# Two-block sequence model: the end of the first channel mixer worked off by token halves, its sums of squares taken on four column groups

## The chip, the core and the metric

The kernel runs on one core of a Trainium2 chip. The metric is the device time of one execution in microseconds (us), and the figure for a kernel is the median of its runs. The core has a matrix engine (TensorE, PE in the profile; its weight loads are PEld), a vector engine (VectorE, DVE), a scalar engine (ScalarE, ACT), a general engine (GpSimd, POOL), and SyncE (SP), whose queue issues most of the transfers. Each engine works through its own instructions in a fixed order and waits for others by semaphores.

## The reference, cut to what matters

```python
x = first_block(...)   # token mixer, then channel mixer; 16 meta tokens + 1024 tokens, width 1024
y = second_block(x)    # rwkv / attention mixer, then channel mixer
# end of first_block's channel mixer, for 1024 tokens:
y = (gelu(a) * (h @ w_up)) @ w_down          # w_down: 2816 x 1024
x = x + rmsnorm(y, g_post)                   # mean of squares over the 1024 channels of a token
# start of second_block:
h = rmsnorm(x, mix_norm_gain)                # again a mean of squares over the channels
proj = h @ w_in                              # 1536 + 32 + 32 + 96 + 1536 columns
p = p_rwkv + (token_shift(p_rwkv) - p_rwkv) * shift_mix
```

Everything is float32.

## The kernel before

Channels lie on the 128 partitions and tokens along the free dimension, so the 1024 channels of a token are eight tiles `y[0]` to `y[7]` of 128 x 1024 tokens. A float32 product is made as three products in a reduced format (`mm3`, lines 196 to 198: high x high, low x high, high x low), so every operand is split into a high and a low part. A product writes 128 x 512 into a bank of PSUM, and most work goes by the two token halves of `CH2`, here the first half (tokens 0 to 511) and the second.

`down` (line 1153) multiplies by `w_down`. It takes the 22 tiles of 128 hidden channels two at a time; for both halves and all eight output tiles it makes 6 products of 128x512 into a bank, and VectorE adds the bank to `y[j]`. After the last pair the function `each` is called for every tile and half.

`ffn1` (line 1187) then makes the two norms. The sum of squares of a half is formed in two ways. For the first norm, ScalarE squares a tile, GpSimd adds the squares of tiles 0 to 6 up in `acc`, and `add_sums` (line 292) lets TensorE reduce the 128 partitions: four calls with a 128-token block of squares as weights and a single column of ones, so that the sums of tokens come to stand on partitions. `rstd` (line 299) makes the reciprocal root there with some 14 small VectorE instructions, spreads it over a diagonal (`rdg`), and multiplies it back to a row for all partitions with TensorE (line 318). Then follow for each tile of a half: scale by gain and root (VectorE, line 156), add the residual `x1` (GpSimd, line 149), high part of the next input (`xh`, ScalarE), its low part (`xl`, VectorE), the square of the new value and four calls of line 292 for the second norm, and the store to `dx2`. The second norm's root goes into `rs`.

The next stage starts on `xh` and `xl` without its norm, which is multiplied in behind the product: `shifted` (line 1297) projects one column tile (24 products for each half) and multiplies the bank by `rs`. `lora_in` calls it for two column tiles, of 128 and of 32 columns, here the first and the second column tile; `rkv` calls it for twelve more. In this block the projections have two banks.

The order of each engine is set by a scheduler at build time, which moves instructions past each other where data allow; a tile in a pool waits until the last user of its buffer is done.

Of the kernel before, what the change touches and what calls it, by code (L numbers as in the profile page):

```python
# [48 lines left out]
class Build:  # L49
# [1103 lines left out]
    def down(self, hid, w_down, y, last, each=None, after=None, between=None):  # L1153
# [14 lines left out]
        for f in range(0, NF, 2):  # L1168
            fs = [load(f), load(f + 1)]
            end = f == NF - 2  # L1170
            for a, b in last if end else CH2:
                for j in range(KD):
                    ps = self.mm_ps([P, b - a])
                    for i, (g, w) in enumerate(fs):
                        self.mm3(ps, (w[0][:, j, :], w[1][:, j, :]), (g[0][:, a:b], g[1][:, a:b]), i == 0, i == 1)
                    if f == 0:
                        nc.scalar.copy(y[j][:, a:b], ps)
                    else:
                        self.tt(y[j][:, a:b], y[j][:, a:b], ps, ALU.add)
                    if each and end:  # L1180
                        each(j, a, b)
                if after and end:
                    after(a, b)
            if between:
                between(f)

    def ffn1(self, fx):
# [4 lines left out]
        acc = self.slot([P, T2], name="acc", tag="WC")  # L1192
        self.dx2 = self.dram([KD, P, T2], "dx2")
        tot = {}

        def each(j, a, b):

            if j < KD - 1:
                self.square_acc(acc, y[j][:, a:b], j, a, b)
                return  # L1200
            if a not in tot:
                tot[a] = self.sums_ps()
                self.add_sums(tot[a], acc[:, a:b], True, False)
            self.square_sum(tot[a], y[j][:, a:b], False, True)

        self.down(hid, I["w_ffn_down"][0], y, CH2, each)
        rp = [self.rstd(tot[a], b - a, D) for a, b in CH2]
        self.rs = self.slot([P, T2], name="rs", tag="R")
        self.xh, self.xl = [], []
        for i, (a, b) in enumerate(CH2):  # L1210
            tot = self.sums_ps()
            for j in range(KD):
                if j % 2 == 0:
                    x1 = self.slot([P, 2, b - a], name="x1", tag="XE")
                    self.dma(out=x1, in_=self.dx1[j:j + 2, :, a:b].rearrange("j p t -> p j t"))
                if i == 0:
                    self.xh.append(self.slot([P, T2], F32R, "xh", "XH"))
                    self.xl.append(self.slot([P, T2], F32R, "xl", "XL"))
                h, l = self.xh[j][:, a:b], self.xl[j][:, a:b]
                t = y[j][:, a:b]  # L1220
                self.stt(t, t, gp[:, j:j + 1], rp[i], ALU.mult, ALU.mult)
                self.tt(t, t, x1[:, j % 2], ALU.add, eng=nc.gpsimd)
                self.act(h, t, AF.Copy, scale=gm[:, j:j + 1])
                self.stt(l, t, gm[:, j:j + 1], h.bitcast(F32), ALU.mult, ALU.subtract)
                self.square_sum(tot, t, j == 0, j == KD - 1)
                self.dma(out=self.dx2[j, :, a:b], in_=t)
            self.rstd(tot, b - a, D, self.rs[:, a:b])
        self.x = list(zip(self.xh, self.xl))

# [67 lines left out]
    def shifted(self, j0, m, mix):  # L1297

        w = self.wcol(self.I["w_in_2"][0], j0, m)
        p = self.slot([P, T2 + 1], name="p", tag="T")[:m]  # L1300
# [781 lines left out]
def block2(B):  # L2082
# [86 lines left out]
```

## Time and profile before

| | |
|---|---|
| time, median of 3 runs | 3236.83 us (3233.69 to 3240.65) |
| the profiled execution: time, span | 3233.1 us, 3231.4 us |
| mean granted TensorE clock | 0.941 of full speed |
| busy PE, PEld | 3009.3 us (93%), 2678.5 us (83%) |
| busy DVE, ACT, POOL | 2009.6 us (62%), 1142.4 us (35%), 1335.0 us (41%) |

The profile is of one execution. The span runs from its first to its last instruction. An engine's busy time is a share of the whole span, so it says little about one stage; the stretch at hand is the end of the first channel mixer, about 1555 to 1640 us. A granted clock of 1.00 is TensorE's upper level, 2.4 GHz, and 0.50 is its lower level, 1.2 GHz; a figure between them is a mean over a stretch with both.

### The profile page before, as it was taken

The page shows a single profiled execution, that of the slowest core. Times are in us where ns is not written, and L with a number is a line of the kernel's source. Part 1 is how long each engine was busy: PE and PEld are TensorE (multiplying, and loading weights), DVE is VectorE, ACT ScalarE, POOL GpSimd, SP SyncE. Part 2 cuts the span into 40 slices and gives each one's busy share as a digit, 9 for nine tenths or more (in the row PEclk, how much of TensorE's full clock was granted, in tenths as well). Part 3 has the DMA queues.
Part 4 walks back from the last instruction along what each step waited for, and adds up shares of the span by engine and source line. Part 5 has one row for each costly group of instructions (what it writes and reads, how often), then busy time and mean ns, then how long its engine had stood idle before and what let it go on. Part 6 is the DMA issues. An engine that isn't in the chain of part 4 may idle for free.

```text
span 3231.4 us, 52682 instructions
## 1 busy us (share of the span) xinstructions
PE 3009.3 (93%) x20614; PEld 2678.5 (83%) x20614; DVE 2009.6 (62%) x3618; ACT 1142.4 (35%) x2168; POOL 1335.0 (41%) x1291
## 2 busy tenths in 40 slices
PE   7999999989799999999999988788988899999998
PEld 6999998979799999877877776677778788887777
DVE  7556654674676666466776555558656766664666
ACT  3344313334343333311333323424444333334111
POOL 3767310033654444232532365543214744454430
PEclk9999999989799999999899989858998899999999
DMA  5333532335222222432223554533425122224321
GB/s 148 86 94 111 174 98 59 105 101 139 78 66 79 81 82 81 150 104 74 90 95 131 146 126 112 137 99 108 115 98 196 53 85 79 80 83 174 113 85 53
DMA packets 322535, 336.83 MB, mean 104 GB/s; under 512 B 60081, under 2 KB 270734, under 8 KB 322286
## 3 DMA queue, kind: packets, MB, share of 16 engines
q1 hardware_dynamic: 289646, 310.38, 31.0%
q10 hardware_dynamic: 32640, 23.08, 2.3%
q8 instruction: 162, 2.65, 0.3%
q14 instruction: 87, 0.71, 0.1%
HBM read 232.66 MB, written 96.40 MB: 102 GB/s over the span
## 4 chain that ended last, share of the span: by engine, by line
PE 61%; DVE 11%; POOL 7%; issue 5%; DMA 4%; ACT 2%; SPq 2%; ACTq 0%; DVEq 0%; POOLq 0%
PE pm L196 13%; PE pm L197 12%; PE pm L198 12%; PE px L197 5%; PE px L196 5%; PE px L198 5%; POOL fs L149 2%; POOL Z L149 2%; DVE dn L149 2%; SPq L142 2%; PE px L292 1%; DVE t L149 1%; PE pa L1877 1%; DMA M<-dm 1%; PE pc L1604 1%
## 5 line engine op out<-in xcount | busy, mean ns | idle before, releaser
L196 PE MATMUL pm<-xh,whi 128*128 128x512 f32 (+5 forms) x1344 | 446.9, 333 | 14.2 <-DVE th L149 11.5
L198 PE MATMUL pm<-xh,wlo 128*128 128x512 f32 (+5 forms) x1344 | 446.8, 333 | 0.0
L197 PE MATMUL pm<-xl,whi 128*128 128x512 f32 (+5 forms) x1344 | 446.4, 332 | 0.0
L149 DVE TENSOR_TENSOR y<-y,pm 128x512 f32<-128x512 f32 (+1 forms) x336 | 218.1, 659 | 159.4 <-PE pm L198 159.1
L196 PE MATMUL pm<-dn,dn 128*128 128x512 f32 (+1 forms) x736 | 286.0, 389 | 6.5 <-DVE y L149 6.2
L196 PEld LDWEIGHTS pm<-xh,whi 128*128 128x128 f32 (+1 forms) x1344 | 257.8, 192 | 35.8 <-DVE th L149 12.4
L197 PE MATMUL pm<-dn,dn 128*128 128x512 f32 (+1 forms) x736 | 282.4, 384 | 1.3 <-POOL dn L149 1.3
L198 PE MATMUL pm<-dn,dn 128*128 128x512 f32 (+1 forms) x736 | 282.5, 384 | 0.0
L197 PEld LDWEIGHTS pm<-xl,whi 128*128 128x128 f32 (+1 forms) x1344 | 257.6, 192 | 19.7 <-issue 0.9
L198 PEld LDWEIGHTS pm<-xh,wlo 128*128 128x128 f32 (+1 forms) x1344 | 257.8, 192 | 19.1 <-issue 0.5
L149 POOL TENSOR_TENSOR dn<-hid,dn 128x1024 fp32r<-128x1024 f32 x44 | 131.8, 3012 | 250.9 <-ACT dn L1161 250.9
L197 PE MATMUL px<-t,sh 128*128 128x258 f32 (+2 forms) x684 | 218.7, 320 | 6.9 <-DVE t L149 6.8
L196 PE MATMUL px<-t,sh 128*128 128x258 f32 (+2 forms) x684 | 217.2, 318 | 0.4 <-DVE gt L149 0.3
L198 PE MATMUL px<-t,sl 128*128 128x258 f32 (+2 forms) x684 | 216.1, 316 | 0.0
L149 DVE TENSOR_TENSOR wlo<-wraw,whi 128x1024 fp32r<-128x1024 f32 (+2 forms) x114 | 153.9, 1351 | 76.2 <-ACT whi L170 74.7
L196 PEld LDWEIGHTS pm<-dn,dn 128*128 128x128 f32 x736 | 138.2, 188 | 43.7 <-DVE y L149 14.2
L170 ACT CAST whi<-wraw 128x1024 fp32r<-128x1024 f32 (+2 forms) x114 | 103.4, 908 | 185.7 <-PE pm L197 154.8
L197 PEld LDWEIGHTS pm<-dn,dn 128*128 128x128 f32 x736 | 138.4, 188 | 29.9 <-POOL dn L149 1.7
L198 PEld LDWEIGHTS pm<-dn,dn 128*128 128x128 f32 x736 | 138.2, 188 | 30.0
L170 ACT CAST dn<-wd 128x1024 fp32r<-128x1024 f32 x44 | 46.1, 1048 | 290.8 <-PE pm L197 290.3
L197 PEld LDWEIGHTS px<-t,sh 128*128 128x128 f32 x684 | 131.3, 192 | 17.9 <-DVE t L149 9.1
L149 POOL TENSOR_TENSOR wraw<-wraw,par 128x1024 f32<-128x1024 f32 (+1 forms) x36 | 73.4, 2041 | 169.0 <-DMA wraw<-in_w_in_dram 128.7
(600 smaller groups left out, 8788.6 us busy)
## 6 DMA issues: line engine op xcount, KB each, us to landing
wraw<-in_w_in_dram SPq DMA_DIRECT2D x61, 512.0 KB
dhid<-up SPq DMA_DIRECT2D x44, 512.0 KB
wd<-in_w_ffn_down_dram SPq DMA_DIRECT2D x44, 512.0 KB
hid<-dhid SPq DMA_DIRECT2D x44, 512.0 KB
wra<-in_w_ffn_up_dram SPq DMA_DIRECT2D x33, 512.0 KB
wrb<-in_w_ffn_up_dram SPq DMA_DIRECT2D x33, 512.0 KB
dg<-th SPq DMA_DIRECT2D x16, 514.0 KB
wraw<-in_w_out_dram SPq DMA_DIRECT2D x16, 512.0 KB
```

What stands on the lines that cost most here:

```text
L142: self.nc.sync.dma_start(out=out, in_=in_)
L149: (eng or self.nc.vector).tensor_tensor(out=o, in0=a, in1=b, op=op)
L170: self.nc.scalar.copy(hi, src)
L196: nc.tensor.matmul(ps, a[0], b[0], start=start, stop=False, **kw)
L197: nc.tensor.matmul(ps, a[0], b[1], start=False, stop=False, **kw)
L198: nc.tensor.matmul(ps, a[1], b[0], start=False, stop=stop, **kw)
L292: self.nc.tensor.matmul(ps[:bw, i:i + 1], src[:, i * bw:i * bw + bw], self.ones[:, 0:1], start=start and i == 0, stop=stop and i == n - 1)
L1604: nc.tensor.matmul(ps, w[:, k], (yh, yl, yh)[q][:, a:b], start=i == 0, stop=i == 11)
L1877: nc.tensor.matmul(self.po[:, i - 4 * ch], pT[:, i * P - a:i * P - a + P], self.vx[j % 2][:, k].rearrange("p e v -> p (e v)")[:, 2 * e:2 * ...
```

## The change

In `down`, the last two pairs of hidden tiles are taken together where `each` is given: first both pairs for the first half, each in its own accumulation, then all four tiles in one accumulation of 12 products for the second half. `each` is so called for the first half while the second half's 96 products are still to come, and a new `after` makes the first half's root and scales its tiles there. The residual (`update`) of both halves stays behind `down`, and its addition goes from GpSimd to VectorE.

Squares are summed in another way for both norms (`square_quarter`): the weights are 32 columns of ones, the moving operand is the 128x512 square, and the result goes to 32 partitions of a bank at the column group 32*(j % 4), so that tiles 0 and 4 share a group. `quarters` copies that bank (ScalarE) and reduces it over the partitions with the four calls of line 292; the sum is 32 times too large, which the divisor 32*D takes back. GpSimd adds no squares up any more.

`shifted` takes several column tiles and goes by halves over all of them. `lora_in` takes its two tiles and the first tile of `rkv` in one call. The 32-column weights have their own loader (`narrow`), and `lora_in` stands ahead of `lora_weights`.

```diff
+        def chunk(fs, a, b, first, end):
+            for j in range(KD):
+                ps = self.mm_ps([P, b - a])
+                for i, (g, w) in enumerate(fs):
+                    self.mm3(ps, (w[0][:, j, :], w[1][:, j, :]), (g[0][:, a:b], g[1][:, a:b]), i == 0, i == len(fs) - 1)
...
+                if each and end:
+                    each(j, a, b)
+            if after and end:
+                after(a, b)
+
+        joint = 4 if each else 0
+        for f in range(0, NF - joint, 2):
...
+        if joint:
+            (a, b), *others = last
+            fs = [load(f) for f in (NF - 4, NF - 3)]
+            chunk(fs, a, b, False, False)
+            more = [load(f) for f in (NF - 2, NF - 1)]
+            chunk(more, a, b, False, True)
+            for a, b in others:
+                chunk(fs + more, a, b, False, True)
...
+        def scaled(j, a, b):
+            t = y[j][:, a:b]
+            self.stt(t, t, gp[:, j:j + 1], rp[a], ALU.mult, ALU.mult)
+
+        def update(j, a, b, x1, ps):
+
+            t = y[j][:, a:b]
+            self.tt(t, t, x1[:, j % 2], ALU.add)
+            h, l = self.xh[j][:, a:b], self.xl[j][:, a:b]
+            self.act(h, t, AF.Copy, scale=gm[:, j:j + 1])
+            self.stt(l, t, gm[:, j:j + 1], h.bitcast(F32), ALU.mult, ALU.subtract)
+            self.square_quarter(ps, t, j)
+            self.dma(out=self.dx2[j, :, a:b], in_=t)
 
         def each(j, a, b):
...
+            if j == 0:
+                sums[a] = self.q_ps([P, b - a])
+            self.square_quarter(sums[a], y[j][:, a:b], j)
+
+        def after(a, b):
+
+            rp[a] = self.rstd(self.quarters(sums[a]), b - a, 32 * D)
+            if a == 0:
+                for j in range(KD):
+                    scaled(j, a, b)
+
+        self.down(hid, I["w_ffn_down"][0], y, CH2, each, after)
...
+                if a:
+                    scaled(j, a, b)
+                update(j, a, b, x1, ps)
+            self.rstd(self.quarters(ps), b - a, 32 * D, self.rs[:, a:b])
         self.x = list(zip(self.xh, self.xl))
+
+    def square_quarter(self, ps, src, j):
+
+        n = src.shape[1]
+        sq = self.small([P, 512], tag="sq", bufs=self.nsq)[:, :n]
+        self.act(sq, src, AF.Square)
+        r = 32 * (j % 4)
+        self.nc.tensor.matmul(ps[r:r + 32], self.ones[:, :32], sq, start=j < 4, stop=j >= KD - 4, tile_position=(0, r))
+
+    def quarters(self, ps):
+
+        n = ps.shape[1]
+        s = self.small([P, 512], tag="sq", bufs=self.nsq)[:, :n]
+        self.nc.scalar.copy(s, ps)
+        tot = self.sums_ps()
+        self.add_sums(tot, s, True, True)
+        return tot
...
+    def shifted(self, *specs):
...
+        for c in CH2:
+            for (j0, m, _, _), w, p in zip(specs, ws, pp):
+                self.proj(w, self.x, [c], lambda ci, a, b, ps: self.tt(p[:, 1 + a:1 + b], ps, self.rs[:m, a:b], ALU.mult), m=m)
...
-        l1 = self.shifted(1536, P, self.par["mix_lora"][:, 0:1])
+        l1, l2, self.key0 = self.shifted((1536, P, self.par["mix_lora"][:, 0:1], "A"), (1664, 32, self.mixl[:, 0:1], "A"),
+                                         (512, P, self.par["mix"][:, 4:5], "T"))
...
+        B.lora_in()
         B.lora_weights()
-        B.lora_in()
```

Three places show what the scheduler makes of it on TensorE. The first is among the last products of `down`, in the kernel before (line 292: sums of the first half; `dn`: operands of `down`):

```order
L198 MATMUL pm_2047_16013<-dn_15867,dn_15870 128x512
L292 MATMUL px_2038_15960<-ones_71,acc_14331 128x1 x4
L292 MATMUL px_2038_15960<-ones_71,sq_15965 128x1 x4
L196 MATMUL pm_2045_16002<-dn_15855,dn_15857 128x512
L197 MATMUL pm_2045_16002<-dn_15856,dn_15857 128x512
```

The same place in the changed kernel, at the last tile of the second half (line 1259: a square summed on a column group, here of the second half; `px_2038`: the first half's root on its way back to a row):

```order
L196 MATMUL pm_2054_16060<-dn_15703,dn_15705 128x512
L1259 MATMUL px_2040_15954<-sq_16023,ones_71 32x512
L197 MATMUL pm_2054_16060<-dn_15704,dn_15705 128x512
L198 MATMUL pm_2054_16060<-dn_15703,dn_15706 128x512
L318 MATMUL px_2038_15927<-rdg_15925,ones_71 128x128 x4
L196 MATMUL pm_2054_16060<-dn_15715,dn_15717 128x512
L1259 MATMUL px_2040_15954<-sq_16040,ones_71 32x512
L197 MATMUL pm_2054_16060<-dn_15716,dn_15717 128x512
```

Between the products of `down` now stand 15 instructions of line 1259 (eight for the first half, seven for the second), the first half's total and its root; the two groups of line 292 are gone from there.

The second place is the product by which the second half's root comes back to a row, in the kernel before (`px_2063`; `px_2065`: the second norm's sums of the first half; `pm_2127`: the first column tile's first half):

```order
L292 MATMUL px_2065_16112<-ones_71,sq_16177 128x1 x4
L292 MATMUL px_2065_16112<-ones_71,sq_16190 128x1 x2
L318 MATMUL px_2063_16106<-rdg_16104,ones_71 128x128 x4
L292 MATMUL px_2065_16112<-ones_71,sq_16190 128x1 x2
L292 MATMUL px_2065_16112<-ones_71,sq_16205 128x1 x4
L292 MATMUL px_2065_16112<-ones_71,sq_16218 128x1 x4
L197 MATMUL pm_2127_16431<-xl_16157,whi_16426 128x512
```

In the changed kernel (`px_2061`; `px_2078`: the same sums; `pm_2132`: the same column tile and half):

```order
L196 MATMUL pm_2132_16382<-xh_16114,whi_16363 128x512
L1259 MATMUL px_2078_16123<-sq_16177,ones_71 32x512
L197 MATMUL pm_2132_16382<-xl_16122,whi_16363 128x512
L198 MATMUL pm_2132_16382<-xh_16114,wlo_16364 128x512
L1259 MATMUL px_2078_16123<-sq_16184,ones_71 32x512
L318 MATMUL px_2061_16102<-rdg_16100,ones_71 128x128 x4
L292 MATMUL px_2092_16190<-ones_71,sq_16188 128x1 x4
L1259 MATMUL px_2097_16219<-sq_16226,ones_71 32x512
```

The root of the second half stood ahead of 14 of the column tile's 24 products and of the last sums; it now stands behind all 24 and behind all eight sums of the first half.

The third place is the end of the second half's sums for the second norm, before (`px_2098`) and after (`px_2097`; `pm_2128`: first column tile, second half; `pm_2133`: second column tile, first half):

```order
L292 MATMUL px_2098_16249<-ones_71,sq_16328 128x1 x4
L318 MATMUL px_2097_16243<-rdg_16241,ones_71 128x128 x4
L292 MATMUL px_2098_16249<-ones_71,sq_16339 128x1 x4
L196 MATMUL pm_2128_16457<-xh_16143,whi_16426 128x512
L197 MATMUL pm_2128_16457<-xl_16144,whi_16426 128x512
```

```order
L1259 MATMUL px_2097_16219<-sq_16280,ones_71 32x512
L1259 MATMUL px_2097_16219<-sq_16288,ones_71 32x512
L292 MATMUL px_2111_16294<-ones_71,sq_16292 128x1 x4
L196 MATMUL pm_2133_16408<-xh_16107,nw_16369 32x512
L197 MATMUL pm_2133_16408<-xl_16115,nw_16369 32x512
L318 MATMUL px_2096_16213<-rdg_16211,ones_71 128x128 x4
```

In both kernels the dense products of the next stage begin behind the second half's last square: six products of `pm_2128` stood ahead of that before, none of `pm_2133` does now, and the total (`px_2111`) has come between.

## Rows read from the trace of the kernel before

**Rows 1.** Stages: us, busy (instructions) by engine, granted clock, DMA share, GB/s

```profile
1560.00:1580.00 20.00, 20.00 (x96) 16.41 (x94) 11.01 (x28) 7.63 (x13) 12.66 (x10) 1.00 0.00 1
1580.00:1600.00 20.00, 15.79 (x81) 14.08 (x80) 18.69 (x33) 11.17 (x18) 14.57 (x11) 0.72 0.63 210
1600.00:1620.00 20.00, 20.00 (x103) 18.74 (x104) 17.82 (x33) 11.06 (x18) 12.66 (x9) 0.67 0.47 162
1620.00:1640.00 20.00, 20.00 (x81) 14.07 (x82) 14.66 (x53) 5.12 (x7) 8.63 (x22) 0.76 0.10 28
...
2100.00:2150.00 50.00, 42.70 (x487) 37.71 (x488) 25.47 (x72) 11.40 (x25) 30.55 (x85) 0.57 0.32 86
```

**Rows 2.** PE in order of time, last products: start, us, engine, line, tiles [idle <-releaser]

```profile
1572.75 0.95 PE L292 MATMUL px<-ones,acc 128*128 128x1 f32 x8
...
1574.45 0.48 PE L196 MATMUL pm<-dn,dn 128*128 128x512 f32 x1
...
1579.85 0.40 PE L198 MATMUL pm<-dn,dn 128*128 128x512 f32 x1
1580.68 1.16 PE L318 MATMUL px<-rdg,ones 128*128 128x128 f32 x8 [0.43 <-DVE rdg L149]
...
1585.34 0.79 PE L196 MATMUL pm<-xh,whi 128*128 128x512 f32 x1
1585.93 3.50 PE L292 MATMUL px<-ones,sq 128*128 128x1 f32 x16
```

**Rows 3.** PE in order of time, from the second half's root on

```profile
1599.76 2.08 PE L318 MATMUL px<-rdg,ones 128*128 128x128 f32 x8 [2.22 <-DVE rdg L149]
1601.63 4.26 PE L292 MATMUL px<-ones,sq 128*128 128x1 f32 x20
...
1606.33 0.63 PE L198 MATMUL pm<-xh,wlo 128*128 128x512 f32 x1
...
1609.50 0.40 PE L197 MATMUL pm<-xl,whi 128*128 128x512 f32 x1
...
1623.65 0.77 PE L196 MATMUL pm<-xh,whi 128*128 128x512 f32 x1
...
1630.20 0.40 PE L197 MATMUL pm<-xl,whi 128*128 128x512 f32 x1
...
1631.79 0.40 PE L197 MATMUL pm<-xl,whi 128*32 128x512 f32 x1
```

**Rows 4.** PE in order of time, a float32 product of 512 columns (line 1362)

```profile
1672.83 1.02 PE L1362 MATMUL pc<-rm,blk 128*128 128x512 f32 x2
1673.68 1.03 PE L1678 MATMUL pq<-ident,mask 128*128 128x128 f32 x8
```

**Rows 5.** PE in order of time, products at tile positions (line 1429)

```profile
1818.75 0.40 PE L198 MATMUL pm<-xh,wlo 128*128 128x512 f32 x1
1819.08 0.76 PE L1429 MATMUL pq<-pr,pr 64*32 64x32 f32 x64
1819.77 0.51 PE L1390 MATMUL pa<-sl,lw 96*128 96x256 f32 x2
```

**Rows 6.** DVE in order of time: a small one, scalings, low part, 1024-wide addition

```profile
1575.04 0.16 DVE L308 COPY rst<-px 128x4 f32<-128x4 f32 x1
...
1581.96 5.36 DVE L156 SCALAR_TENSOR_TENSOR y<-y,par,px 128x512 f32<-128x512 f32 x8 [0.74 <-ACT sq L159]
...
1597.03 0.74 DVE L156 SCALAR_TENSOR_TENSOR xl<-y,par,xh 128x512 fp32r<-128x512 f32 x1
...
1644.08 1.21 DVE L149 TENSOR_TENSOR wlo<-wraw,whi 128x1024 fp32r<-128x1024 f32 x1
```

**Rows 7.** ACT in order of time: a square, a high part, a copy from PSUM

```profile
1585.19 0.61 ACT L159 ACTIVATE sq<-y 128x512 f32<-128x512 f32 x1
1585.80 0.72 ACT L159 ACTIVATE xh<-y,par 128x512 fp32r<-128x512 f32 x1
...
1622.33 0.58 ACT L320 COPY rs<-px 128x512 f32<-128x512 f32 x1 [1.46 <-PE px L318]
```

**Rows 8.** POOL in order of time: the first half's residual additions

```profile
1583.26 11.73 POOL L149 TENSOR_TENSOR y<-y,x 128x512 f32<-128x512 f32 x8
```

More of the change, by code (lines that the diff above doesn't have):

```diff
@@ L1166, in load @@
             return (gh, gl), (wh, wl)
-        for f in range(0, NF, 2):
+        def chunk(fs, a, b, first, end):
[3 more added lines that the diff above has]
+                    self.mm3(ps, (w[0][:, j, :], w[1][:, j, :]), (g[0][:, a:b], g[1][:, a:b]), i == 0, i == len(fs) - 1)
+                if first:
+                    nc.scalar.copy(y[j][:, a:b], ps)
+                else:
+                    self.tt(y[j][:, a:b], y[j][:, a:b], ps, ALU.add)
+                if each and end:
[4 more added lines that the diff above has]
+        for f in range(0, NF - joint, 2):
             fs = [load(f), load(f + 1)]
@@ L1171, in down @@
             for a, b in last if end else CH2:
[L1172 to L1183, printed above, removed]
+                chunk(fs, a, b, f == 0, end)
             if between:
                 between(f)
+        if joint:
[6 more added lines that the diff above has]
+                chunk(fs + more, a, b, False, True)
     def ffn1(self, fx):
@@ L1206, in ffn1, with residual @@
[L1206 to L1211, printed above, removed]
+        self.rs = self.slot([P, T2], name="rs", tag="R")
+        rp, sums = {}, {}
+        (a0, b0), (a1, b1) = CH2
+        def residual(j, a, b):
+            x1 = self.slot([P, 2, b - a], name="x1", tag="XE")
+            self.dma(out=x1, in_=self.dx1[j:j + 2, :, a:b].rearrange("j p t -> p j t"))
+            return x1
@@ new lines, in each @@
+        def each(j, a, b):
+            if j == 0:
[7 more added lines that the diff above has]
+        self.down(hid, I["w_ffn_down"][0], y, CH2, each, after)
+        self.xh, self.xl = ([self.slot([P, T2], F32R, n, t) for _ in range(KD)] for n, t in (("xh", "XH"), ("xl", "XL")))
@@ L1212, in ffn1 @@
+        for a, b in CH2:
+            ps = self.q_ps([P, b - a])
             for j in range(KD):
                 if j % 2 == 0:
[L1214 to L1227, printed above, removed]
@@ L1295, in out_gate, with narrow @@
                 self.dma(out=self.dbon[j, :, 1, a:b], in_=t)
[L1297 to L1306 removed]
+    def shifted(self, *specs):
+        ws, pp, res = [], [], []
+        for j0, m, _, tag in specs:
+            ws.append(self.wcol(self.I["w_in_2"][0], j0, m) if m == P else self.narrow(self.I["w_in_2"][0], j0, m))
+            pp.append(self.slot([P, T2 + 1], name="p", tag=tag)[:m])
+        for c in CH2:
+            for (j0, m, _, _), w, p in zip(specs, ws, pp):
+                self.proj(w, self.x, [c], lambda ci, a, b, ps: self.tt(p[:, 1 + a:1 + b], ps, self.rs[:m, a:b], ALU.mult), m=m)
+        for (j0, m, mix, tag), p in zip(specs, pp):
+            self.ts(p[:, :1], p[:, 1:2], 0.0, ALU.mult)
+            d = self.slot([P, T2], name="d", tag=tag)[:m]
+            self.tt(d, p[:, :T2], p[:, 1:], ALU.subtract, eng=self.nc.gpsimd)
+            self.stt(d, d, mix, p[:, 1:], ALU.mult, ALU.add)
+            res.append(d)
+        return res
+    def narrow(self, src, c0, m):
+        raw, hi, lo = (self.slot([P, KD, m], dt, "nw", "W") for dt in (F32, F32R, F32R))
+        self.dma(out=raw, in_=src[:, c0:c0 + m].rearrange("(k p) m -> p k m", p=P))
+        self.split_to(hi, lo, raw)
+        return hi, lo
     def lora_in(self):
         self.dlora = self.dram([160, T2], "dlora")
[L1311 removed]
+        l1, l2, self.key0 = self.shifted((1536, P, self.par["mix_lora"][:, 0:1], "A"), (1664, 32, self.mixl[:, 0:1], "A"),
+                                         (512, P, self.par["mix"][:, 4:5], "T"))
         self.act(l1[:32], l1[:32], AF.Tanh)
```

22 lines of the change are left out of this document (5 added, 17 removed).

## The prediction

> **What bounds the kernel now.** I read the stages first, then TensorE in order of time, then the engines that it waits for. Up to the last product of `down` TensorE is full: 20.00 us busy of 20 at a granted clock of 1.00 [rows 1]. From the first product after the first half's sums to the last product 23 steps take 5.40 us, 0.235 us each [rows 2], so the last one is through at 1580.1. Then the clock falls to 0.72, 0.67 and 0.76 for three stretches of 20 us [rows 1], and the next stage's dense products begin only at 1623.65, behind the second half's last sum [rows 3]. These 43.5 us are the stage to look at. They divide at 1601.84, where the second half's root is back as a row (1599.76 and 2.08 us) [rows 3]: 21.7 us before it, 21.8 us behind it. TensorE does little useful work there, but it is not free: it is the engine that makes every sum of squares, in program order, and at the lower clock a product lasts 0.63 us where it lasts 0.40 at the upper one [rows 3]. What stands ahead of the last product of `down` costs its full length, what stands behind it costs only where it makes the chain longer. That is the measure for the change, which shortens the chain but puts work ahead of the last product.
>
> **The sums among the products.** Fifteen instructions of line 1259 come to stand among the products. Line 1362 is the nearest row: a float32 product of 512 moving columns, two records, and the next instruction starts 0.85 us later [rows 4]. Its weights are 128 columns wide, those of line 1259 only 32. That this shortens nothing is seen on products of the three-part kind, 0.40 us at 128 and at 32 columns [rows 3]. Each such instruction also stands between products that use the whole array. Where products at tile positions follow a full product, the first starts 0.33 us behind it and not 0.235 [rows 5], so I add 0.10 us and take 0.95 us. Fifteen make 14.3 us. With them come the first half's total, half of the two groups of line 292 (1.70 us from 1572.75 to 1574.45 [rows 2]), 0.85 us, and its root's product, about 1.0 us (1.16 us with its pipeline [rows 2]). The two groups themselves go, 1.7 us. Sum: 14.3 + 0.85 + 1.0 - 1.7 = 14.4 us later for the last product, at 1594.5. From below the bound is an instruction that overlaps its neighbours, as the 64 of line 1429 do, which take 0.69 us together, 0.011 each [rows 5]: nearly nothing, and then 15 of them cost perhaps 0.25 us each, one product's step. From above it is 1.15 us each, 17.3 us. I stay at 0.95, since line 1362 has the same shape and type and no partner ran beside it.
>
> The page "TensorEngine Tiling (Array Packing)" of the Trainium skill, section Key Properties, speaks against this place: changing the tiling mode drains the engine. If each of the 30 changes of mode cost the tail of a product (0.40 - 0.235 = 0.165 us), the sum would be 12.75 + 5.0 + 0.15 = 17.9 us instead of 14.4; the row shows 0.10 us for one change.
>
> **Up to the second half's root.** In VectorE's order the first half's eight scalings and two residual additions stand ahead of the last addition from PSUM. Let r be the end of the first half's root product on TensorE; behind it stand nine products and two instructions of line 1259, 4.0 us, so r is 1590.5. Eight scalings take 5.36 us [rows 6], three additions 0.6 each (half of the 1.21 us of a 1024-wide one [rows 6]), the square 0.61 [rows 7], line 1259 0.95, the copy 0.58 [rows 7], the total 0.85: TensorE can begin the first half's eight sums for the second norm at r + 10.5, at the lower clock at r + 12. Behind them in its order stand the column tile's remaining 23 products and only then the second half's root. At the upper clock that is 8 x 0.95 + 23 x 0.235 = 13.0 us and 1.0 for the root's product, r + 24.5; at the lower clock all doubles, r + 38. VectorE's part, which the root also needs, is done by r + 20 (5.4 + 9 x 0.6 + 8 x 0.7 + 14 x 0.2 + 0.7 for `rdg`), so TensorE's queue decides. Which clock? Between 1580.1 and 1585.34 TensorE idled for 0.43 us and more and worked little, and from 1585.93 on two groups of sums last 3.50 us, the lower level [rows 2]; the clock was up again at 1609.50, after work without a gap since 1599.76 [rows 3]. The new order has the same lull, waiting for the scalings. I let the lower clock hold until r + 21, 9 us into the run of sums: 9 of 24.2 us are done, the rest takes 8.2 us, and the root is there at r + 30, or 1620.5. Before it was there 21.7 us behind the last product, now 26: 4.3 us more, with bounds of -1.2 and +12.3.
>
> The addition on VectorE instead of GpSimd (11.73 us for eight [rows 8]) is a real gain for the chain: 0.6 us each. But the place where TensorE's queue is late hides it.
>
> **From the root to dense products.** Scalings 5.4 us, the first addition 0.6, then ScalarE makes eight high parts and eight squares, 8 x 0.72 + 8 x 0.61 = 10.6 [rows 7], the last line 1259 0.95 to 1.8, copy 0.6, total 0.85 to 1.7: 19.0 to 20.7. I take 20.5 at the lower clock, against 21.8 before: -1.3, bounds -2.8 and +2 (where the eight sums at 1.7 us each run one after the other). The second column tile's weights come from a transfer that is queued on SyncE behind the last store, and so behind the last addition, at root + 13; it has some 7 us to land, which I take as hidden; if not, it adds up to 3 us.
>
> **What costs nothing.** Eight additions from PSUM fewer lie under full TensorE. Behind the restart 120 products are left until `rkv` goes on as before, in both kernels (24 + 48 + 48 then, 24 + 24 + 24 + 24 + 24 now). The residual's loads, three of them ahead, have the same buffers and the same places between the stores as before. The later stages are shuffled by the scheduler too; I have no row to size that and allow 6 us either way in the range.
>
> **Sum.** 14.4 + 4.3 - 1.3 = 17.4 us. The profiled execution took 3233.1 us (span 3231.4, 1.7 us around it), so 3250.5 on its own scale. It lies 3.7 us under the median, 3236.83, on whose scale the sum is 3254. I predict 3252, between the two, since the three runs spread over 7 us.
>
> **The rivals.**
>
> *Cheap sums, faster.* If a column group really runs beside the products, line 1259 costs about 0.25 us, the last product is 3.9 us late, r is 2.6 us ahead of it, the chain of VectorE alone decides (root at r + 21, 18.4 us behind the last product, -3.3), the second part saves 2.8, and the clock that falls no more saves some 3 of the 6 us for which it was low between 1623.65 and 1630.20 [rows 3]: -5.2, some 3232. The 0.69 us of 64 instructions [rows 5] speaks for it; that those stand next to each other at different positions, while here a full product stands on either side, against. It decides where the price falls below 0.5 us. The same page, section Theoretical Speedup, gives up to four times for 32 columns; that needs four in a row, which only the second half's last eight have.
>
> *Upper clock throughout.* If the sums count as work and the clock stays up, 14.4 - 1.2 - 2.8 - 3 = +7.4, some 3244. [...] Against: the lull of 7 us remains.
>
> *Lower clock throughout.* 14.4 + 12.3 + 2 = +29, some 3266, if the gaps between the squares keep it down as from 1585 to 1609.
>
> *Given back later.* The stage from 1800 to 2200 waits for chains more than for products, and at 2100 to 2150 its clock is 0.57 [rows 1]; column tiles that come later can fill it. If the delay is swallowed there, the time stays near 3238. Against: the stretch between is full TensorE again.
>
> **How the numbers follow.** This kernel's measurement tells 0.2%, 6.5 us, from no change. Forecast 0.55, all but a tenth of it slower, the rest the same. Cheap sums 0.09, half of it faster by more than 0.2%. Upper clock 0.15, two thirds slower. Lower clock 0.11, slower. Given back 0.10, mostly the same, a third faster through the shuffled order. Together: slower 0.71, same 0.21, faster 0.08. The range runs from 3237, which leaves out the cheap sums and half of what is given back, to 3266, the lower clock; about 0.18 lies outside.
>
> **What would show it.** In TensorE's rows of the changed kernel: line 1259 among the products of `down` with 0.9 to 1.0 us to the next start, and the last product near 1594.5; line 318 for the second half some 26 us behind that, directly behind the 24th product of the first column tile; the 32-column products starting near 1641. GpSimd shows no additions there, VectorE's take 0.6 us. The prediction is wrong if line 1259 starts its successor within 0.5 us, if the granted clock there is 1.00, or if dense products start before 1630.

## The result and the profile after

The changed kernel takes 3274.7 us (median of 4 runs, 3273.5 to 3276.5), the kernel before beside it 3235.3 us. The ratio is 1.0118, 95% interval 1.0105 to 1.0131: 1.2% slower, and 23 us above the forecast of 3252. Its profiled execution has a span of 3272.8 us, 41.4 us more than before.

The stages after, in the columns of [rows 1], read first:

```profile
1560.00:1580.00 20.00, 20.00 (x81) 12.12 (x80) 5.22 (x16) 3.53 (x6) 0.00 (x0) 1.00 0.00 0
1580.00:1600.00 20.00, 16.65 (x58) 8.55 (x56) 12.97 (x23) 4.42 (x7) 0.00 (x0) 0.94 0.14 41
1600.00:1620.00 20.00, 19.32 (x63) 8.70 (x62) 9.53 (x26) 8.62 (x15) 0.00 (x0) 0.80 0.46 170
1620.00:1640.00 20.00, 12.54 (x42) 3.94 (x42) 19.21 (x47) 11.26 (x20) 3.23 (x10) 0.74 0.54 168
1640.00:1660.00 20.00, 20.00 (x92) 13.70 (x91) 7.84 (x26) 2.74 (x4) 3.43 (x8) 1.00 0.01 2
...
1680.00:1700.00 20.00, 16.35 (x66) 12.96 (x65) 17.80 (x22) 3.76 (x5) 6.49 (x5) 0.91 0.25 79
1720.00:1740.00 20.00, 14.90 (x49) 10.01 (x48) 11.69 (x13) 9.64 (x12) 5.53 (x2) 0.83 0.52 179
1740.00:1760.00 20.00, 16.01 (x52) 10.93 (x51) 9.46 (x12) 7.76 (x8) 6.18 (x3) 0.83 0.23 81
```

The lull around 1580 to 1640 is still there, and three gaps are new: in three stretches between 1680 and 1760 TensorE idles 12.7 us of 60, and the granted clock averages 0.83 in two of them. In the kernel before, the stretches from 1660 to 1780 that have any gap are these (TensorE alone), with 3.7 us of idle time in all at a clock of 1.00:

```profile
1660.00:1680.00 20.00, 19.05 (x83) 1.00 0.32 106
1720.00:1740.00 20.00, 18.32 (x76) 1.00 0.26 94
1760.00:1780.00 20.00, 18.97 (x87) 1.00 0.47 148
```

TensorE of the changed kernel in order of time, for [rows 2, 3]:

```profile
1550.45 0.40 PE L198 MATMUL pm<-dn,dn 128*128 128x512 f32 x1
1550.78 1.05 PE L1259 MATMUL px<-sq,ones 128*32 128x512 f32 x2
1551.76 0.50 PE L196 MATMUL pm<-dn,dn 128*128 128x512 f32 x1
1552.09 0.40 PE L197 MATMUL pm<-dn,dn 128*128 128x512 f32 x1
...
1554.73 1.05 PE L1259 MATMUL px<-sq,ones 128*32 128x512 f32 x4
1555.71 0.50 PE L196 MATMUL pm<-dn,dn 128*128 128x512 f32 x1
...
1592.93 0.40 PE L198 MATMUL pm<-dn,dn 128*128 128x512 f32 x1
1593.25 1.04 PE L1259 MATMUL px<-sq,ones 128*32 128x512 f32 x2
...
1618.34 1.16 PE L318 MATMUL px<-rdg,ones 128*128 128x128 f32 x8
1619.33 0.95 PE L292 MATMUL px<-ones,sq 128*128 128x1 f32 x8
1626.89 8.97 PE L1259 MATMUL px<-sq,ones 128*32 128x512 f32 x16 [6.61 <-ACT sq L159]
...
1637.45 0.39 PE L196 MATMUL pm<-xh,nw 128*32 128x512 f32 x1
...
1693.57 0.77 PE L196 MATMUL pm<-xh,whi 128*128 128x512 f32 x1 [3.65 <-DVE p L149]
...
1727.93 2.08 PE L1418 MATMUL pc<-rm,blk 128*128 128x512 f32 x2 [5.10 <-ACT rm L159]
```

The last product of `down` starts at 1592.9 (before 1579.85), the dense products at 1637.45 (before 1623.65). So at the restart the change is 13.8 us late; the other 27.6 us of the 41.4 are lost behind it.

The table cuts every profiled execution at two places: the start of the last product of `down`, and the issue of the first store to `dm`, with which the first of the eight rwkv units begins. The three stretches make the span. The times are compared with runs of the kernel before made beside them, whose medians were 3235 to 3241. The stretches are of one execution each, and that execution lay up to 6 us from the median of its kernel (short sums, new start: 3269.6 against 3263.7); the kernel before spread from 3229.6 to 3245.6. So a few us in one of these columns can be the execution and not the edit.

| kernel | time / before (95%) | last product | to first `dm` | from there to the end |
|---|---|---|---|---|
| before | 1 | 1579.9 | 240.3 | 1411.2 |
| after | 1.0118 (1.0105-1.0131) | 1592.9 | 257.7 | 1422.2 |
| new end, old start | 1.0057 (1.0041-1.0073) | 1592.7 | 246.4 | 1418.7 |
| old end, new start | 1.0017 (1.0004-1.0029) | 1582.9 | 252.0 | 1409.0 |
| old sums, new start | 1.0029 (1.0018-1.0039) | 1582.4 | 257.2 | 1400.6 |
| old sums, old start | 1.0002 (0.9991-1.0013) | 1582.3 | 244.1 | 1413.7 |
| residual on VectorE | 1.0046 (1.0028-1.0065) | 1581.4 | 251.7 | 1415.0 |
| short sums, new start | 1.0079 (1.0066-1.0093) | 1586.0 | 252.6 | 1429.2 |
| short sums, old start | 1.0021 (1.0008-1.0035) | 1583.1 | 242.2 | 1413.6 |
| the same, residual on GpSimd | 1.0021 (1.0009-1.0032) | 1583.1 | 244.1 | 1418.4 |
| tables first | 1.0057 (1.0041-1.0073) | 1595.3 | 256.7 | 1407.6 |
| key apart | 1.0101 (1.0085-1.0117) | 1594.7 | 255.8 | 1420.7 |
| weights first | 1.0113 (1.0098-1.0128) | 1593.6 | 261.6 | 1412.4 |
| key apart, tag T | 1.0083 (1.0062-1.0104) | 1595.8 | 249.8 | 1420.8 |
| old start, tag A | 1.0089 (1.0069-1.0109) | 1595.8 | 260.2 | 1412.9 |
| rotary, other data | 1.0103 (1.0082-1.0125) | 1593.9 | 256.7 | 1420.0 |
| before, short sums | 0.9989 (0.9978-0.9999) | 1582.9 | 241.8 | 1411.2 |
| before, short sums, start in tag T | 0.9954 (0.9936-0.9972) | 1581.3 | 240.7 | 1401.2 |
| before, start in tag T | 1.0011 (0.9999-1.0023) | 1580.3 | 246.6 | 1416.2 |
| old sums, start in tag T | 1.0100 (1.0082-1.0118) | 1580.4 | 247.2 | 1437.6 |

### The profile page after: what moved, and what is told of

The parts are those of the page before. It is cut to its first block, busy times and chain, and to the rows that moved or that the text cites. A ratio compares the mean times of both kernels' runs of the same rounds, so it can differ in the third digit from the quotient of the medians.

```text
span 3272.8 us, 52501 instructions
## 1 busy us (share of the span) xinstructions
PE 3025.9 (92%) x20550; PEld 2660.2 (81%) x20550; DVE 1996.5 (61%) x3626; ACT 1141.9 (35%) x2171; POOL 1293.1 (40%) x1263
## 4 chain that ended last, share of the span: by engine, by line
PE 61%; DVE 11%; POOL 6%; issue 5%; DMA 4%; ACT 2%; SPq 1%; DVEq 0%; ACTq 0%; POOLq 0%
PE pm L196 13%; PE pm L197 13%; PE pm L198 12%; PE px L197 5%; PE px L196 5%; PE px L198 5%; POOL Z L149 2%; POOL fs L149 2%; DVE dn L149 2%; SPq L142 1%; PE pa L1933 1%; PE pc L1580 1%; DVE t L149 1%; PE px L292 1%; PE pc L1660 1%
## 5 line engine op out<-in xcount | busy, mean ns | idle before, releaser
L196 PE MATMUL pm<-xh,whi 128*128 128x512 f32 (+4 forms) x1328 | 442.7, 333 | 17.3 <-DVE th L149 10.9
L197 PE MATMUL pm<-xl,whi 128*128 128x512 f32 (+4 forms) x1328 | 442.0, 333 | 0.1
L198 PE MATMUL pm<-xh,wlo 128*128 128x512 f32 (+4 forms) x1328 | 441.6, 333 | 0.0
L196 PEld LDWEIGHTS pm<-xh,whi 128*128 128x128 f32 x1328 | 257.2, 194 | 38.2 <-DVE th L149 11.6
L197 PEld LDWEIGHTS pm<-xl,whi 128*128 128x128 f32 x1328 | 257.2, 194 | 24.6 <-issue 3.4
L198 PEld LDWEIGHTS pm<-xh,wlo 128*128 128x128 f32 x1328 | 257.1, 194 | 18.0 <-issue 0.5
L149 DVE TENSOR_TENSOR sl<-ss,sh 128x512 fp32r<-128x512 f32 x88 | 95.0, 1080 | 80.0 <-ACT sh L170 79.9
```

The lines of the kernel that those rows point to most:

```text
L149: (eng or self.nc.vector).tensor_tensor(out=o, in0=a, in1=b, op=op)
L196: nc.tensor.matmul(ps, a[0], b[0], start=start, stop=False, **kw)
L197: nc.tensor.matmul(ps, a[0], b[1], start=False, stop=False, **kw)
L198: nc.tensor.matmul(ps, a[1], b[0], start=False, stop=stop, **kw)
```

## The experiments

### The end and the start of the change, apart

**New end, old start.** `shifted`, `lora_in`, `rkv` and the order of the calls as before the change.

> The changed end of the first channel mixer, with the old start of the second block: shifted by one column tile at a time, lora_weights ahead of lora_in, the first key tile in rkv, no narrow loader. Theory A (the new start of the second block loses the time behind the restart): the restart is still about 14 us late, what came behind it goes, time 3249 us (3243 to 3256), first line-1362-type product of the removal about 14 us later than before. Theory B (a restart that is late shuffles the later stages whatever the start looks like): 3268 to 3278 us, as the changed kernel.

3257.4 us. The last product of `down` stays late (1592.7), and up to the first `dm` 11.3 us came back. That is the direction of theory A and not its size: the time is a microsecond above A's range, and the removal's first product comes 18.9 us later than before (1691.7 against 1672.8) where A had about 14.

**Old end, new start**, the other half of the diff.

> The old end of the first channel mixer, with only the new start of the second block. Theory A: dense products restart at about 1624 us as before, but the three column tiles go by halves, VectorE's small work for the rotary tables and the mask stands behind them and TensorE stalls in the removal: 3253 to 3262 us. Theory B: 3229 to 3241 us, no change.

3242.7 us, between both ranges. The stretch to the first `dm` is 11.7 us longer than before, with the waits of the changed kernel (TensorE 3.6 us for VectorE's `p`, then 5.1 us for ScalarE's `rm`); 2 us came back behind it, which one execution cannot tell from nothing.

**Old sums, new start.**

```diff
-            self.square_quarter(sums[a], y[j][:, a:b], j)
+            self.square_acc(acc, y[j][:, a:b], j, a, b)   # tiles 0 to 6; tile 7 and total by line 292
...
-            self.square_quarter(ps, t, j)
+            self.square_sum(ps, t, j == 0, j == KD - 1)
```

> The changed kernel with the squares summed as before: GpSimd adds the squares of seven tiles, four calls of line 292 reduce them; the second norm by four calls of line 292 for each tile; everything else as changed (no line 1259 anywhere). Theory A: fifteen sums of 0.98 us leave the products of down, the last product comes at about 1580 instead of 1595, and the time falls by 10 to 16 us, to 3259 to 3265 us. Rival C (the sums are paid in the tail either way, since the 32 small calls for the second half are back): under 5 us of it is seen, 3270 to 3278 us.

3245.0 us, 30 below the changed kernel and far under both ranges. The last product came at 1582.4, as A says, 10.5 us earlier, and to the first `dm` it took as long as with the new sums. The rest, 21.6 us, came behind it, where this edit changes no instruction.

**Old sums, old start**: halves and the early first root alone are left.

> Only what is left of the changed end when its sums go back: the last two pairs together by halves, the first half's root and scalings behind the products, residual on VectorE, but squares summed as before and the old start of the second block. Theory A (terms add): 3245 (changed kernel with old sums) less 17 (old start, as it gave with the new sums) = 3228 us, 3222 to 3234. Theory B (the new start costs 5 to 7 us, as it did on the old end, and the old start holds the two banks through the tail): 3236 to 3243 us.

3238.0 us, no change: theory B. On every one of these ends the new start lengthens the stretch to the first `dm`, by 11.3, 11.7 and 13.1 us.

### The price of a sum

**Short sums**, with either start (one record of 0.24 us in place of two):

```diff
-        sq = self.small([P, 512], tag="sq", bufs=self.nsq)[:, :n]
+        sq = self.small([P, 512], F32R, tag="sq", bufs=self.nsq)[:, :n]
-        self.nc.tensor.matmul(ps[r:r + 32], self.ones[:, :32], sq, ..., tile_position=(0, r))
+        self.nc.tensor.matmul(ps, self.onesr, sq, start=j == 0, stop=j == KD - 1)
```

> The changed kernel with its sums of squares as one short product each: squares and ones are rounded to the reduced format (which leaves precision out), 128 columns of ones, one record per sum, all eight tiles in one accumulation; the divisor becomes 128*D. Places and order stay. Theory A (each term costs its own length): 15 sums of 0.24 instead of 0.98 us, the last product 11 us earlier, 3260 to 3265 us. Theory B (what is lost behind the restart depends on how the later stages come to stand): the same 11 us earlier at the last product, but the total anywhere between 3243 and 3275 us, with the stage of eight units (first store of dm to last store of dyn) different by 5 us or more from the changed kernel's 386.

> As the kernel with short sums (squares and ones in the reduced format), with the old start of the second block. Theory A: 11 to 13 us less than the kernel with the changed end and the old start (3257): 3244 to 3246 us. Theory B: the last product 11 us earlier, the total anywhere from 3232 to 3257 us.

3263.7 and 3243.0 us: 11 and 14 us less, near theory A both times, one within and one a microsecond under its range; theory B's wide ranges hold both totals too. The last product comes at 1586.0 and 1583.1 instead of 1592.9 and 1592.7, 7 and 10 us earlier where 11 were expected. The difference between the two lies ahead of the sums: from the first sum to the last product it is 32.6 and 32.7 us (from 1553.4 and 1550.4) instead of 42.1 and 42.2 (from 1550.8 and 1550.5), 9.5 us less both times. What the sums cost ahead of the last product is so shown; that the totals fell by about that is partly luck, since the last stretch moved by +7.0 and -5.1 us in the two (of the first, 5.8 us are the profiled execution's distance from its median).

### The residual on VectorE

```diff
-                self.tt(t, t, x1[:, j % 2], ALU.add, eng=nc.gpsimd)
+                self.tt(t, t, x1[:, j % 2], ALU.add)
```

> The kernel before, with only the addition of the residual on VectorE instead of GpSimd. Theory A: eight additions of 1.47 us on GpSimd become eight of 0.6 us on VectorE in the chain from the second half's root to the restart, which is 3 to 7 us earlier: 3228 to 3232 us. Rival: VectorE's own queue or TensorE's sums are as late, 3233 to 3238 us.

3251.6 us, 0.46% slower; both theories fell. TensorE's queue in order of time:

```profile
1601.65 6.82 PE L292 MATMUL px<-ones,sq 128*128 128x1 f32 x32
1608.33 0.77 PE L197 MATMUL pm<-xl,whi 128*128 128x512 f32 x1
1608.90 1.91 PE L318 MATMUL px<-rdg,ones 128*128 128x128 f32 x8
```

The second half's root comes at 1608.90 instead of 1599.76 [rows 3]. Four tiles of sums (16 calls, 32 records) now go ahead of the root, at the lower clock; behind it stood 20 records of them before. A likely reason, not tested, is that with faster additions the first half's squares are ready early in the scheduler's order. With the old sums, halves and the old start the same addition is in a kernel that loses nothing (3238.0). A quicker operation in a chain went together with other work moving in front of it.

### What the new start waits for

**Tables first.** If VectorE's small work for the rotary tables and the mask is what delays the removal, its calls can go ahead:

```diff
+        B.rotary_tables()
+        B.attn_mask()
         B.lora_in()
         B.lora_weights()
-        B.rotary_tables()
-        B.attn_mask()
```

> The changed kernel with rotary_tables and attn_mask called ahead of lora_in. Theory A (behind the restart VectorE's small work stands between the first key tile and its removal, and TensorE waits for both): the first product of the removal (line 1418 in the changed kernel) comes 45 to 55 us behind the restart instead of 69, the removal's last within 130 us, and the time falls by 8 to 14 us, to 3261 to 3267 us. Rival: the removal is not what the later stages wait for, 3270 to 3280 us.

3257.0 us, but not in the way expected: the removal's first product came 61 us behind the restart, its last 141. The later waits are gone, and in their place stands one for the first bank (VectorE and TensorE in order of time):

```profile
1663.45 0.69 DVE L153 TENSOR_SCALAR e<-c 128x1024 f32<-128x1024 f32 x1
1664.05 0.69 DVE L149 TENSOR_TENSOR p<-pm,rs 128x512 f32<-128x512 f32 x1
...
1664.79 0.80 PE L196 MATMUL pm<-xh,whi 128*128 128x512 f32 x1 [16.90 <-DVE p L149]
```

`p`, whose row `rs` was there at 1644.3, is written only once the mask's work on `f`, `e`, `c` is nearly through. The total is below both ranges; the gain lies in the last stretch (14.6 us), not here (256.7 instead of 257.7).

**Key apart**, or **weights first** (`lora_weights` ahead of `lora_in` again, the edit of one line):

```diff
-        l1, l2, self.key0 = self.shifted((1536, ..., "A"), (1664, ..., "A"), (512, ..., "T"))
+        l1, l2 = self.shifted((1536, ..., "A"), (1664, ..., "A"))
...
-                if (i, j) == (1, 0):
-                    t = self.key0
```

> The changed kernel with the first key tile back in rkv: shifted takes only the two tiles of lora_in by halves, all else as changed. Theory A (with three tiles by halves, all their mixes come late, and VectorE's small work then stands between the first key tile and its removal): from the last product of down to the first store of dm 244 to 250 us instead of 258, no wait of the removal's product for ScalarE of 5 us; the time falls by 8 to 14 us, to 3260 to 3267, if the stage of the units stays as it is. Theory B (the narrow loader or the place of lora_weights is to blame): 255 to 260 us, 3270 to 3278 us.

> The changed kernel with lora_weights ahead of lora_in, as before. Theory A (the joining of three tiles is to blame): from the last product to the first store of dm 255 to 260 us, time 3268 to 3278 us. Theory B (the place of lora_weights): 244 to 250 us, 3258 to 3266 us.

3271.0 and 3272.8 us. The first falls out as theory B of its text, the second as theory A of its own (its 261.6 us to the first `dm` are 1.6 above A's range), so each points at the other: neither part alone gives the time back. What both kept is the last argument of the two tiles, the tag: `"A"` instead of `"T"`. Tag A has three buffers in this block (`A=3`), and `rotary_tables` (`ex`, `rw`), `distance_mask` (`f`, `e`, `c`) and `removal` (`kk`, `sq`, `rn`) take theirs from it. VectorE in order of time, in the changed kernel and then before:

```profile
1660.25 1.29 DVE L156 SCALAR_TENSOR_TENSOR d<-d,par,p 128x1024 f32<-128x1024 f32 x1 [1.79 <-POOL d L149]
...
1666.46 0.15 DVE L153 TENSOR_SCALAR ex<-ff 128x1 f32<-128x1 f32 x1 [0.53 <-DMA dlora<-d]
...
1672.74 1.28 DVE L156 SCALAR_TENSOR_TENSOR d<-d,par,p 128x1024 f32<-128x1024 f32 x1
...
1697.47 0.74 DVE L153 TENSOR_SCALAR rm<-d,par 128x1024 f32<-128x1024 f32 x1
```

```profile
1628.60 0.15 DVE L153 TENSOR_SCALAR ex<-ff 128x1 f32<-128x1 f32 x1
...
1666.03 0.75 DVE L153 TENSOR_SCALAR rm<-d,par 128x1024 f32<-128x1024 f32 x1
```

The first small instruction of the tables, `ex`, waits for the store to `dlora`. No data join the two, only the buffer does. It starts 29.0 us behind the restart (before 5.0). The removal needs buffers of the same tag: the key tile is mixed at 1674.0, its removal starts at 1697.5.

**Tag T instead of A, and A in the old start.** The same kernel as with the key apart, with one letter changed twice; and the new end with the old start, with the opposite edit.

```diff
-        l1, l2 = self.shifted((1536, P, ..., "A"), (1664, 32, ..., "A"))
+        l1, l2 = self.shifted((1536, P, ..., "T"), (1664, 32, ..., "T"))
```

> The changed kernel with the first key tile back in rkv (as the run with the key apart, 3271 us), and the two tiles of lora_in in the buffers of tag T, as before the change, instead of tag A. Theory A (rotary_tables, distance_mask and the removal wait for the buffers of tag A): VectorE's first ex comes within 10 us of the restart instead of 29, the removal's product waits under 2 us for ScalarE, from the last product of down to the first store of dm 243 to 249 us instead of 256, time 3256 to 3265 us. Rival (going by halves is what costs): 254 to 258 us, 3267 to 3275 us.

> The changed end with the old start (3257 us), but the two tiles of lora_in in the buffers of tag A; nothing goes by halves. Theory A (buffers of tag A): from the last product of down to the first store of dm 253 to 260 us instead of 246, time 3264 to 3272 us. Rival: 245 to 249 us, 3254 to 3261 us.

Tag T instead of A: 6.0 us less to the first `dm` (249.8 against 255.8 with the key apart) and 3266.2 us, each a microsecond above A's range; the time is also a microsecond under the rival's. Tag A in the old start: 13.8 us more (260.2 against 246.4, at the upper end of A's range), time 3268.4, within A's range and 11 more than with tag T. With the key apart `ex` starts 23.2 us behind the restart and waits for the store to `dlora` (0.52 us); with tag T it starts 8.4 us behind it. The first removal's start on VectorE moves by about as much as the stretch, from 1692.8 to 1686.9 and, in the old start, from 1684.9 to 1698.5. How long TensorE waits for removals (us in total, times, longest), first with the key apart and tag A, with T, and last in the old start with A, where with T there is no such wait:

```profile
PE pc L1415 <- ACT rm L159: 7.6, 1, 7.6
PE pc L1415 <- ACT rm L159: 1.9, 1, 1.9
PE pc L1402 <- ACT rm L159: 7.8, 2, 7.5
```

So the buffers are shown as a cause, in both directions and on both starts: in each pair nothing but the tag differs. For the size, two kernels with the same code up to there (the changed one, and the one with other data for the rotary, below) differ by 1.0 us in this stretch.

### The stages behind

In the changed kernel VectorE stands still for 10.0 us in the middle of a unit, and TensorE behind it:

```profile
2053.09 1.23 DVE L149 TENSOR_TENSOR ro<-ro,rot 128x1024 f32<-128x1024 f32 x1 [10.04 <-DMA ro<-dqkv]
...
2054.84 1.59 PE L1552 MATMUL pc<-LR 32*96 32x96 f32 x8 [9.52 <-DVE A L149]
```

**Rotary, other data**, in `rotary`:

```diff
-            self.dma(out=a[16 * k:16 * k + 16], in_=rows[k, :16])   # and two more loads
+            self.dma(out=a[16 * k:16 * k + 16], in_=other[k, :16])  # other: the same view of drkv
```

> The changed kernel with the rotary's 24 loads reading drkv, which is complete by then, instead of dqkv (the values are then not the attention's; what is left out is that these loads wait for the projection's store). Theory A (VectorE's wait of 10.0 us for the second tile's loads lengthens the stage of the units): no wait of VectorE for ro of over 2 us, first store of dm to last store of dyn 371 to 378 us instead of 386, time 3260 to 3267 us. Rival (the length of that stage comes from where its other work stands): 382 to 390 us, 3270 to 3279 us.

The kernel so leaves out the wait of these loads for the attention's own projection, and its result is not the program's. 3273.2 us: the rival. VectorE's wait for the second tile fell to 0.43 us, and the units' stage by 8 us, as theory A says, but what comes behind it grew by 6; from the first `dm` to the end it is 1420.0 against 1422.2 us. Here a wait of 10 us was not 10 us of time.

### Versions

**Before, short sums; the same, start in tag T.** The kernel before with the second norm's sums as short products (as above), and then also with the start of the kernel "key apart, tag T".

```diff
-                self.square_sum(tot, t, j == 0, j == KD - 1)
+                self.square_quarter(ps, t, j)   # rounded square, 128 columns of ones
```

> The kernel before, with only the second norm's sums as short products (squares and ones in the reduced format, one product of 128 columns of ones per tile, one accumulation, divisor 128*D) instead of four calls of line 292. Theory A (TensorE's sums bound the tail: sixteen groups of 0.9 to 1.7 us become 0.24 to 0.5 us): the tail is 6 to 14 us shorter, 3222 to 3230 us. Rival (the chain over VectorE, GpSimd and ScalarE bounds it): 3232 to 3238 us.

> The kernel before with short sums of the second norm (3234.7 us), and the new start with the key apart and the lora tiles in tag T. Theory A (without the conflict over tag A, going by halves costs nothing and lets the banks go earlier): 3226 to 3234 us. Rival (with halves 24 products less are at hand for the tail): 3236 to 3244 us.

3234.7 us (ratio 0.9989, hardly to be told from before; the rival) and 3224.1 us (0.9954, two below A's range). The second beats both kernels, but by nothing that its edit aims at: up to the first `dm` it takes as long as before (240.7), and its gain is in the last stretch, 1401.2 instead of 1411.2. A run of the short sums in the old start with the residual back on GpSimd took 3243.3 us, as with VectorE (3243.0); 3235 to 3240 had been expected if VectorE's additions hold up the root, 3247 to 3251 if the chain through the additions decides, and neither came.

**Before, start in tag T; old sums, start in tag T**, both at full precision.

> The kernel before with only the start by halves over two column tiles, lora tiles in tag T, key tile in rkv, lora_in ahead of lora_weights; sums of squares as before. Theory A (the start makes the gain): 3220 to 3230 us, and from the last product of down to the first store of dm 238 to 243 us. Theory B (the gain is the length of the stages behind, which no edit steers; over the kernels run it went from 1400 to 1429 us): up to the first store of dm as before, the total anywhere between 3228 and 3245 us.

> The changed kernel with the squares summed as before (3245 us) and the start by halves over two tiles in tag T. Theory A (buffers of tag A cost 6 to 12 us wherever they are): from the last product to the first store of dm 245 to 251 us instead of 257, total 3232 to 3240 us. Rival: the sum of the terms is hidden by the stages behind, 3241 to 3250 us.

3243.4 and 3270.4 us. The second is the clearest case of all: to the first `dm` it takes 247.2 us instead of 257.2, as theory A says, and yet it is 25 us slower than the kernel it was made from, outside both ranges, because the stages behind took 1437.6 instead of 1400.6 us. The start in tag T is no gain of its own: the first of the two is within theory B's range in its total, and 6 us longer than before up to the first `dm` (246.6), which neither theory had.

## Why the prediction was wrong

**The sums among the products: right in size, wrong in make.** I had 15 instructions of 0.95 us, 14.4 us in all with the rest. The last product came 13.0 us later; over the eight kernels with these sums it stands at 1592.7 to 1595.8, over the nine with the old ones at 1579.9 to 1582.9. Two errors cancel. A sum between products delays the stream by 1.17 us, above my upper bound: 0.33 before it, 0.98 to the next start, 0.33 behind, less two steps of 0.235. But the fifteenth sum starts behind the last product (1593.25), not between the products as I had read the order, and six of the others stand in pairs, and a pair on two column groups takes 0.98 us (x4, 1554.73 to 1555.71) like one: eleven places ahead of the last product, not fifteen. 11 x 1.17, 0.9 for the total, 1.0 for the root, less 1.7, make 13.1.

**Up to the second half's root: right.** Forecast 26 us from the last product to the root as a row; measured 1592.9 to 1619.5 (1618.34 and 1.16), 26.6. The clock fell and rose about as I drew it: products take 0.63 us at 1604.98 and again 0.40 from 1608.15, 18 us behind the first half's root (1590.05), where I had 21. (A slip in the working: my terms up to the first half's sums add to 10.2 us, not 10.5; they began 12.5 us behind that root, and I had 12 at the lower clock.)

**From the root to dense products: right in sign, too long.** Forecast 20.5 us, at least 19.0; measured 18.0, 3.8 less than before. ScalarE's high part and square come every 1.13 us (squares at 1628.49 and 1629.62), not 1.33, and the granted clock was up again at 1631.7, where I had the lower one to the end. So the restart is 13.8 us late where I had 17.4.

**What costs nothing: the step that failed.** I wrote that nothing is lost behind the restart because the same number of products is left, and allowed 6 us for the shuffled stages. Measured are 27.6 us, in two parts.

16.6 us are lost by the first `dm`. I counted TensorE's work, not who holds the buffers. The diff moves the two lora tiles from tag T to tag A, whose three buffers the tables, the mask and the removal need next. The tag alone is worth 6.0 and 13.8 us in the two pairs that differ in nothing else. From the changed kernel back to the one before, by one step at a time, the stretch from the last product shrinks by 1.9 us (key apart), 6.0 (tag T), 3.4 (old start) and 6.1 (old end), 17.4 together; the tag is the largest single cause shown in the start, and with tag T the start by halves still costs 3 to 6 us on three of the four ends that had it (nothing on the old end with short sums), for a reason that no run shows. The 6.1 us are the new end with the old start (246.4 against 240.3). There TensorE's next instruction is the second norm's root, and it waits for it; no run isolates this wait:

```profile
1647.98 2.08 PE L318 MATMUL px<-rdg,ones 128*128 128x128 f32 x8 [5.29 <-DVE rdg L149]
```

11.0 us are lost from the first `dm` to the end (some 2 us less on the scale of the medians). No edit here touches that code, other than the one to the rotary's loads, but each leaves the scheduler to set it in another order. Over all kernels that stretch took 1400.6 to 1437.6 us, and two with the same start lie 22 us apart (1400.6 and 1422.2). My 6 us had no row behind it and should have been some 20 either way. Where the time goes can be read: TensorE runs the same 8724 instructions there in every kernel of the table, and between the two extremes, old sums with the new start and with the start in tag T, its idle time grows from 111.2 to 125.8 us and its busy time from 1289.5 to 1311.8, at a mean granted clock of 0.92 and 0.91. From before to after idle time grows by 4.2 and busy time by 6.8 us. What in the order makes it so is open: the one long wait that I took away (10 us) moved the total by 2.

**The rivals.** None describes the result. The lower clock's 3266 came nearest in size, by a mechanism that is not there; the time was not given back later either, more was lost.

## What to carry to other kernels

When an edit gives a tile another buffer tag, list everyone who takes a buffer of that tag next, and what must finish before it is free: a load, a mask or a table with no data in common can wait for your store. In a program whose order a scheduler sets, judge an edit by the stretch it touches, cut at fixed instructions, and take the spread of the untouched stretches from other variants before reading a total: here it was up to 37 us, nearly three times the largest effect of a tag (13.8).

## What the runs showed of the hardware

Two float32 sums of 512 columns, one right behind the other on two column groups, take the time of one (0.98 us, 1554.73 above). The Trainium skill's page "TensorEngine Tiling (Array Packing)", section Theoretical Speedup, gives up to four times where a dimension is at most 32; the trace agrees for two in a row, and in no run here do more than two start together. Eight in a row took 8.97 us (1626.89 above), because ScalarE handed them over one by one, every 1.13 us:

```profile
1628.49 0.61 ACT L159 ACTIVATE sq<-y 128x512 f32<-128x512 f32 x1
1629.01 0.70 ACT L159 ACTIVATE xh<-y,par 128x512 fp32r<-128x512 f32 x1
1629.62 0.61 ACT L159 ACTIVATE sq<-y 128x512 f32<-128x512 f32 x1
```

On both sides of a sum between full products the step to the next instruction is 0.33 us instead of 0.235, 0.19 us for each place. The same page of the Trainium skill, section Key Properties, says that a change of tiling mode drains the engine; these steps are in line with it, though no run separates a drain from other causes.
